# The low parts of the keys in a forgetting attention: 64 rows of the array for each head, in one tile for two heads

## The chip, the cores and the metric

The kernel runs on one core of a Trainium2 chip. The metric is the device time of one execution in microseconds (us): the median of the runs shown. A profile records one further execution, instruction by instruction, for the engines TensorE (PE, with its weight loads listed apart as PEld), VectorE (DVE), ScalarE (ACT), GpSimd (POOL) and SyncE (SP, which issues transfers).

## The reference

One layer of a hybrid encoder on 512 frames of width 1024, in float32. One input projection feeds eight heads of forgetting attention and four heads of a gated linear recurrence; both are put together by `w_out`; a cross attention over 256 memory tokens and a squared-ReLU network follow. Only the attention is touched:

```python
def fox_attention(q, k, v, log_f):
    nb = s_ // Q_BLOCK
    scale = 1.0 / math.sqrt(d_)
    F = jnp.cumsum(log_f, axis=-1)
    def block(args):
        qi, Fi, pi = args
        s = jnp.einsum('bhqd,bhkd->bhqk', qi, k).astype(jnp.float32) * scale
        s = s + Fi[..., None] - F[:, :, None, :]
        mask = pi[:, None] >= key_pos[None, :]
        s = jnp.where(mask, s, -jnp.inf)
        p = jax.nn.softmax(s, axis=-1)
        return jnp.einsum('bhqk,bhkd->bhqd', p.astype(v.dtype), v)
    out = lax.map(block, (qb, Fb, pos))
```

There are 8 heads of width 64, 512 frames and query blocks of 128 frames. Block tb sees the keys of the first (tb + 1) × 128 frames.

## The kernel before

**Numbers in two parts.** Products run in the format fp32r, which the kernel makes up for by splitting each operand into a high part (a copy in fp32r, on ScalarE) and a low part (the rest, by a subtraction on VectorE). A projection is the sum of three products: high by high, high by low, low by high (`gemm_fm`, L236 to L238, and `gemm_tm`, L249 to L251).

**Heads in pairs.** The eight heads go in four pairs p, with j = 0 or 1 inside a pair. `fox_proj(p)` (L733) projects the queries and the keys of a pair, 64 features of head 0 on partitions 0 to 63 and 64 features of head 1 on partitions 64 to 127. From the queries it makes one tile `q` for each head, in which the 64 rows of the head (the slice `r`) hold the high part and the other 64 rows (`r2`) the low part (L743, L744). From the keys it makes `kh`, with two halves by j: half j has the high part of head j on both sets of rows (L755, L756). A single product over 128 rows, q by kh, thus adds high by high and low by high. The tile `kl` has two halves too: half j holds the low part of head j on its own 64 rows (L757) and zeros on the other 64, which GpSimd writes (L748). The product q by kl over 128 rows adds high by low; the rows of the low queries meet zeros.

**Scores.** `fox_scores(p, tb)` (L924) takes both heads in turn: a bank `ps` of the pool `sc` (two buffers), the product with kh (L930), the product with kl (L931), each 128 rows by 128 stationary columns, the queries of the block, with n = 128, 256, 384 or 512 moving columns, the keys; then `fox_softmax` (L934): VectorE subtracts and takes the row's extreme (L941), ScalarE exponentiates and sums (L943), VectorE inverts and scales (L944, L945). GpSimd has prepared the bias and the mask in the tile `bi` (`fox_bias`, L915).

**The loop.** 16 steps over (pair, block) at L991. Step n transposes the probabilities of step n - 1 (`fox_T`, L953), on odd steps multiplies earlier ones by the values (`fox_out`, L969, outputs of 64 columns for each of the two heads), computes the scores of step n, has the biases of step n + 1 made and then runs a measured portion of other work, `fill.run`: the next pair's projections and the keys and values of the memory. The amounts, in microseconds, stand in `FX` (L37).

**Order.** TensorE's instructions stand in the order in which they are written out. The other engines' order is planned by the framework, with the priorities that `ahead` sets.

Two earlier pieces use other shapes on TensorE: the recurrence's products with 64 stationary columns (L629, L699) and two small transpositions, one of 33 rows (`l_soft`, L468) and four with 8 columns (`gate_rows`, L662).

Of the kernel before, what the change touches and what calls it, by code (L numbers as in the profile page):

```python
# [10 lines left out]
R = mybir.dt.float32r  # L11
U8 = mybir.dt.uint8
AF = mybir.ActivationFunctionType
ALU = mybir.AluOpType
# [3 lines left out]
S = 512  # L18
# [24 lines left out]
def emit(  # L43
# [22 lines left out]
    te, ve, ac, gp = nc.tensor, nc.vector, nc.scalar, nc.gpsimd  # L66
# [29 lines left out]
    def k4(shape, name, dt=F32):  # L96
        return k4p.tile([P] + shape, dt, tag="k4", name=name)

    def q2(name):
        return q2p.tile([P, S], R, tag="q2", name=name)  # L100

    def t3(name):
        return t3p.tile([P, S], F32, tag="t3", name=name)

    def t2(name, dt=F32, shape=(S,)):
        return t2p.tile([P] + list(shape), dt, tag="t2", name=name)
# [6 lines left out]
    def mm(name, shape=(S,)):  # L113
        return mmp.tile([P] + list(shape), F32, tag="mm", name=name)
# [4 lines left out]
    def sc(name, shape=(S,)):  # L119
        return scp.tile([P] + list(shape), F32, tag="sc", name=name)  # L120
# [4 lines left out]
    def f(a):  # L125
        return a.bitcast(F32)
# [85 lines left out]
    def next_panel():  # L212
        while len(stream) < min(state["used"] + 2, len(specs)):
            for split in load_next():
                with ahead(PW):
                    split()
        r = stream[state["used"]]
        state["used"] += 1
        return r
# [9 lines left out]
    def gemm_fm(ps, wt, col, ahi, alo, n=S, order=range(KC), begun=False):  # L229

        whi, wlo = wt
        sl = slice(col, col + P)
        for n_, k in enumerate(order):
            hi, lo = chunk(ahi, k, slice(0, n)), chunk(alo, k, slice(0, n))
            wh, wl = chunk(whi, k, sl), chunk(wlo, k, sl)
            te.matmul(ps, wh, hi, start=n_ == 0 and not begun, stop=False)  # L236
            te.matmul(ps, wh, lo, start=False, stop=False)  # L237
            te.matmul(ps, wl, hi, start=False, stop=k == order[-1])  # L238
            yield 3 * n / 2400
# [322 lines left out]
    for hp in range(2):  # L562
        wt = next_panel()
        for j in range(2):
            h = 2 * hp + j
            ps = mm(f"gq{h}")
# [115 lines left out]
    for li, m in enumerate(mlev):  # L682
# [8 lines left out]
        for hp in range(2):  # L691
# [3 lines left out]
            ps = sc(f"lv{hp}{m}", (NT, 2, w))  # L695
# [35 lines left out]
    fq, fk = {}, {}  # L731

    def fox_proj(p):  # L733
        wt = next_panel()

        fq[p] = [q2(f"q{p}{j}") for j in range(2)]
        ps = mm(f"pq{p}")
        yield from gemm_fm(ps, wt, 0, hn_hi, hn_lo)
        t = t3(f"qs{p}")
        ve.scalar_tensor_tensor(t, ps, 0.125, rbc, op0=ALU.mult, op1=ALU.mult)  # L740
        for j in range(2):
            r, r2 = slice(64 * j, 64 * j + 64), slice(64 - 64 * j, 128 - 64 * j)
            ac.activation(fq[p][j][r, :], t[r, :], AF.Copy)  # L743
            ve.tensor_tensor(fq[p][j][r2, :], t[r, :], f(fq[p][j][r, :]), ALU.subtract)  # L744
        kh, kl = k4([2, S], f"kh{p}", R), k4([2, S], f"kl{p}", R)
        fk[p] = (kh, kl)
        for j in range(2):
            gp.memset(f(kl[64 - 64 * j : 128 - 64 * j, j, :]), 0.0)  # L748
        ps = mm(f"pk{p}")
        yield from gemm_fm(ps, wt, P, hn_hi, hn_lo)  # L750
        t = t3(f"ks{p}")
        ve.tensor_tensor(t, ps, rbc, ALU.mult)
        for j in range(2):
            r, r2 = slice(64 * j, 64 * j + 64), slice(64 - 64 * j, 128 - 64 * j)
            ac.activation(kh[r, j, :], t[r, :], AF.Copy)  # L755
            ac.activation(kh[r2, j, :], t[r, :], AF.Copy)  # L756
            ve.tensor_tensor(kl[r, j, :], t[r, :], f(kh[r, j, :]), ALU.subtract)  # L757

    fill.add(fox_proj(0), "proj0")

    fill.until("gg")
# [58 lines left out]
    for c in range(NT):  # L820
# [24 lines left out]
        with ahead(P1):  # L845
            hs = sm(4, f"hs{c}")
            for h in range(4):
                j = t2(f"hj{c}{h}", F32, (P,))
# [75 lines left out]
    def fox_scores(p, tb):  # L924
        n = (tb + 1) * P
        ts_ = slice(tb * P, n)
        kh, kl = fk[p]
        for j in range(2):
            ps = sc(f"ps{2 * p + j}{tb}")
            te.matmul(ps[:, 0:n], fq[p][j][:, ts_], kh[:, j, 0:n], start=True, stop=False)  # L930
            te.matmul(ps[:, 0:n], fq[p][j][:, ts_], kl[:, j, 0:n], start=False, stop=True)  # L931
            fox_softmax((p, tb, j), ps)

    def fox_softmax(u, ps):  # L934
        p, tb, j = u
        h, n = 2 * p + j, (tb + 1) * P
        with ahead(P3):

            b = prob[u][:, 0:n]
            mx = sm(1, f"mx{h}{tb}")  # L940
            ve.tensor_tensor_reduce(out=b, in0=ps[:, 0:n], in1=b, scale=-1.0, scalar=-NEG, op0=ALU.add, op1=ALU.min, accum_out=mx)  # L941
            den = sm(1, f"dn{h}{tb}")
            ac.activation(b, b, AF.Exp, bias=mx, scale=-1.0, accum_out=den)  # L943
            ve.reciprocal(den, den)  # L944
            ve.tensor_scalar(b, b, den, None, op0=ALU.mult)  # L945
# [45 lines left out]
    for n in range(len(pairs) + 2):  # L991
        if n < len(pairs):
            p, tb = pairs[n]
            if tb == 0:
                fill.until(f"proj{p}")
                if p == 0:
                    fill.add(fox_proj(1), "proj1")
                    fill.add(proj_tm(new_fv(), WT, AF.Identity, "fv"), "fv256")
                elif p == 1:
                    fill.add(fox_proj(2), "proj2")  # L1000
                    for i in range(V0):
                        fill.add(mem_v(i))
                elif p == 2:
                    fill.until("fv256")
                    fill.add(fox_proj(3), "proj3")
                    fill.add(mem_v_wide())
                    fill.add(mem_v(3))
                    for i in range(4):
                        fill.add(mem_k(i))
# [13 lines left out]
        if n < len(pairs):  # L1023
            fox_scores(*pairs[n])
            if n + 1 < len(pairs):
                fox_biases(n + 1)
            if tb == 2 and p < 3:
                fox_rows(p + 1)
# [528 lines left out]
```

## Time and profile before

| what | value |
| --- | --- |
| median of 3 runs | 768.9 us (768.85 to 769.19) |
| profiled execution, own time | 769.28 us |
| profiled execution, span from first to last instruction | 767.5 us |
| mean granted TensorE clock | 0.998 |
| scores with kh (L930), with kl (L931) | 32 products each, 8 for each of four widths |
| fills of zeros (L748) | 8 |

In the prediction's timeline lines the columns are: start in us from the span's first instruction, duration in us (for a group, from its start to its last end, or the sum where they overlap less), engine, line, operation, the tile written and the tiles read, the shape of the array used as rows*columns, the operand's shape, and the number of instructions merged. Durations of TensorE are modelled and overlap one another; the step from one start to the next tells the pace. A bracket tells of idle time of that engine before the line and what ended it; "issue" means that no recorded event ended it. A row of the stretches gives start and end, length, and the busy time and number of instructions of each engine, then the granted clock, the share of the DMA engines and their rate. Rows that group a line show the number of instructions, the shortest, median and longest duration in ns, and the first and the last start.

### The profile page before, as it was taken

The numbers are of one execution on the slowest core, as the hardware profiler recorded it, in microseconds if no ns is written. First come the engines' busy times: TensorE is split into PE (matmuls) and PEld (weight loads), VectorE is DVE, ScalarE is ACT, GpSimd is POOL, SyncE is SP. The second block draws the span as 40 slices with busy tenths as digits, with TensorE's granted clock in tenths as the row PEclk, the third lists the DMA queues.
The fourth block names the chain that finished last, engine by engine and source line by source line (L and its number), as shares of the span: only waits on it lengthen the run. The fifth ranks groups of instructions, "written<-read, shape, count | busy, mean of one in ns | idle before, by whom it ended". The sixth has DMA issues, their size and how long they took to land.

```text
span 767.5 us, 11244 instructions
## 1 busy us (share of the span) xinstructions
PE 759.0 (99%) x4229; PEld 646.0 (84%) x4229; DVE 523.7 (68%) x849; ACT 368.7 (48%) x620; POOL 190.5 (25%) x264
## 2 busy tenths in 40 slices
PE   9999999999999999999999999999999999999996
PEld 6889888998889988888888888888888888888885
DVE  5747765576787656555548556949596868777696
ACT  5655456665666433344444244435353535342553
POOL 7207432423432025310016510101001010101123
PEclk9999999999999999999999999999999999999999
DMA  8543332232543442231113596565748475757602
GB/s 247 192 136 108 90 84 56 80 114 57 185 149 134 163 139 83 85 100 64 56 56 108 204 262 139 146 158 175 180 149 200 139 174 161 192 137 218 138 1 109
DMA packets 79831, 103.03 MB, mean 134 GB/s; under 512 B 4593, under 2 KB 58394, under 8 KB 79778
## 3 DMA queue, kind: packets, MB, share of 16 engines
q1 hardware_dynamic: 70226, 76.61, 31.1%
q0 software_dynamic: 8960, 24.67, 15.3%
q10 hardware_dynamic: 592, 1.05, 0.4%
q8 instruction: 33, 0.54, 0.3%
q14 instruction: 20, 0.16, 0.1%
HBM read 89.71 MB, written 4.21 MB: 122 GB/s over the span
## 4 chain that ended last, share of the span: by engine, by line
PE 98%; DVE 1%; ACT 1%; POOL 0%; issue 0%; DVEq 0%; ACTq 0%
PE u L238 8%; PE u L236 8%; PE u L237 8%; PE U L1371 4%; PE U L1369 4%; PE U L1370 4%; PE xq L236 2%; PE xq L237 2%; PE xw L236 2%; PE xq L238 2%; PE xw L237 2%; PE xw L238 2%; PE wo L236 2%; PE Y L1371 2%; PE wo L238 2%; PE Y L1370 2%
## 5 line engine op out<-in xcount | busy, mean ns | idle before, releaser
L175 DVE TENSOR_TENSOR wld<-wq,whd 128x1024 fp32r<-128x1024 f32 x56 | 68.6, 1226 | 25.3 <-ACT whd L171 25.2
L236 PE MATMUL u<-x_hi,whu 128*128 128x512 f32 x192 | 74.7, 389 | 0.0
L237 PE MATMUL u<-x_lo,whu 128*128 128x512 f32 x192 | 74.7, 389 | 0.0
L238 PE MATMUL u<-x_hi,wlu 128*128 128x512 f32 x192 | 74.7, 389 | 0.0
L171 ACT ACTIVATE whd<-wq 128x1024 fp32r<-128x1024 f32 x56 | 58.4, 1054 | 30.2 <-PE u L237 18.5
L171 ACT ACTIVATE whu<-wru 128x1024 fp32r<-128x1024 f32 x24 | 25.3, 1053 | 62.1 <-DMA wru<-in_w_dram 62.1
L175 DVE TENSOR_TENSOR wlu<-wru,whu 128x1024 fp32r<-128x1024 f32 x24 | 29.5, 1229 | 32.8 <-ACT whu L171 32.8
L1245 POOL DMA_DIRECT2D wq<-in_w_dram x16 | 19.4, 1242 | 129.1 <-DMA wq<-in_w_dram 117.6
L1369 PE MATMUL U<-whd,hb 128*128 128x512 f32 x120 | 46.7, 389 | 0.0
L1370 PE MATMUL U<-wld,hb 128*128 128x512 f32 x120 | 46.7, 389 | 0.0
L1371 PE MATMUL U<-whd,hb 128*128 128x512 f32 x120 | 46.7, 389 | 0.0
L1245 POOL DMA_DIRECT2D wq<-wq x16 | 14.1, 878 | 123.9 <-DVE wld L175 96.3
L237 PEld LDWEIGHTS u<-x_lo,whu 128*128 128x128 f32 x192 | 36.0, 188 | 7.5
L238 PEld LDWEIGHTS u<-x_hi,wlu 128*128 128x128 f32 x192 | 36.0, 188 | 7.5
L236 PEld LDWEIGHTS u<-x_hi,whu 128*128 128x128 f32 x192 | 36.0, 188 | 7.4
L921 POOL TENSOR_SCALAR bi<-nF,Ft 128x128 f32<-128x128 f32 (+3 forms) x32 | 20.6, 654 | 54.6 <-PE pt L953 34.5
L1308 ACT ACTIVATE sq<-ur 128x512 f32<-128x512 f32 x32 | 20.0, 627 | 26.2 <-DVE ur L1305 26.2
L1305 DVE SCALAR_TENSOR_TENSOR ur<-u,rbc 128x512 f32<-128x512 f32 x32 | 21.9, 688 | 11.5 <-PE u L238 11.5
L1370 PEld LDWEIGHTS U<-wld,hb 128*128 128x128 f32 x120 | 22.5, 188 | 4.7
L1371 PEld LDWEIGHTS U<-whd,hb 128*128 128x128 f32 x120 | 22.5, 188 | 4.7
L1369 PEld LDWEIGHTS U<-whd,hb 128*128 128x128 f32 x120 | 22.5, 188 | 4.6
L1070 ACT ACTIVATE x_hi<-hT,gv 128x512 fp32r<-128x512 f32 x16 | 11.5, 719 | 28.5 <-DVE hT L1069 28.4
(961 smaller groups left out, 2364.2 us busy)
## 6 DMA issues: line engine op xcount, KB each, us to landing
wq<-in_w_dram SPq DMA_DIRECT2D x40, 512.0 KB, 3.3
wru<-in_w_dram SPq DMA_DIRECT2D x24, 512.0 KB, 3.8
wq<-in_w_dram POOLq DMA_DIRECT2D x16, 512.0 KB, 8.2
wq<-wq POOLq DMA_DIRECT2D x16, 512.0 KB, 4.6
xTd<-xT POOLq DMA_DIRECT2D x4, 512.0 KB, 3.3
nF<-Fd POOLq DMA_DIRECT2D x8, 256.0 KB, 3.7
hT<-xTd POOLq DMA_DIRECT2D x4, 512.0 KB, 5.4
xt<-in_x_dram SPq DMA_DIRECT2D x3, 512.0 KB
```

The source lines that it names most:

```text
L171: ac.activation(hi, raw, AF.Copy)
L175: ve.tensor_tensor(lo, raw, f(hi), ALU.subtract)
L236: te.matmul(ps, wh, hi, start=n_ == 0 and not begun, stop=False)
L237: te.matmul(ps, wh, lo, start=False, stop=False)
L238: te.matmul(ps, wl, hi, start=False, stop=k == order[-1])
L921: gp.tensor_scalar(bi[:, 0:n], fF[h][:, 0:n], -1.0, Ft[:, tb, h : h + 1], op0=ALU.mult, op1=ALU.add)
L1245: gp.dma_start(raw.rearrange("p (k n) -> p k n", k=2), src, accum_op=ALU.add)
L1305: ve.scalar_tensor_tensor(u, ps, 0.0, rbc2, op0=ALU.max, op1=ALU.mult)
L1308: ac.activation(sqs[g, j][:, i, :], u, AF.Square)
L1369: te.matmul(ps, hi, whi[:, k, :], start=begin, stop=False, skip_group_check=True)
L1370: te.matmul(ps, hi, wlo[:, k, :], start=False, stop=False, skip_group_check=True)
L1371: te.matmul(ps, lo, whi[:, k, :], start=False, stop=k == 1, skip_group_check=True)
```

## The change

`kl` is now one half of its tile, 128 partitions by 512 columns, which both heads share: head 0's low part on partitions 0 to 63, head 1's on 64 to 127. The zeros and GpSimd's eight instructions for them are gone. In `fox_scores` the product with kl takes only the 64 rows of its head, of the queries' tile and of kl. The order of a call is no longer kh, kl of head 0 and kh, kl of head 1, but both banks first, then kh of head 0, kh of head 1, kl of head 0, kl of head 1, and then the two softmaxes.

```diff
-        kh, kl = k4([2, S], f"kh{p}", R), k4([2, S], f"kl{p}", R)
+        kh, kl = k4([2, S], f"kh{p}", R), k4([2, S], f"kl{p}", R)[:, 0, :]
         fk[p] = (kh, kl)
-        for j in range(2):
-            gp.memset(f(kl[64 - 64 * j : 128 - 64 * j, j, :]), 0.0)
...
-            ve.tensor_tensor(kl[r, j, :], t[r, :], f(kh[r, j, :]), ALU.subtract)
+            ve.tensor_tensor(kl[r, :], t[r, :], f(kh[r, j, :]), ALU.subtract)
...
         kh, kl = fk[p]
-        for j in range(2):
-            ps = sc(f"ps{2 * p + j}{tb}")
+        pss = [sc(f"ps{2 * p + j}{tb}") for j in range(2)]
+        for j, ps in enumerate(pss):
             te.matmul(ps[:, 0:n], fq[p][j][:, ts_], kh[:, j, 0:n], start=True, stop=False)
-            te.matmul(ps[:, 0:n], fq[p][j][:, ts_], kl[:, j, 0:n], start=False, stop=True)
+
+        for j, ps in enumerate(pss):
+            r = slice(64 * j, 64 * j + 64)
+            te.matmul(ps[:, 0:n], fq[p][j][r, ts_], kl[r, 0:n], start=False, stop=True)
+        for j, ps in enumerate(pss):
             fox_softmax((p, tb, j), ps)
```

## The prediction

> **What bounds the kernel now.** I read the page first: the span, the busy shares, the granted clock and the chain that ended last.
>
> ```profile
> span 767.5 us, 11244 instructions
> ...
> PE 759.0 (99%) x4229; PEld 646.0 (84%) x4229; DVE 523.7 (68%) x849; ACT 368.7 (48%) x620; POOL 190.5 (25%) x264
> ...
> PEclk9999999999999999999999999999999999999999
> ...
> PE 98%; DVE 1%; ACT 1%; POOL 0%; issue 0%; DVEq 0%; ACTq 0%
> ```
>
> TensorE is busy for 99% of the span at its full granted clock, and 98% of the chain lies on it. The stretch of the change is the loop over (pair, query block) at L991, from about 140 to 262 us; its busy times by engine are one row, and the list of TensorE's waits between 100 and 700 us is one other:
>
> ```profile
> 140.00:262.00 122.00, 122.00 (x900) 110.20 (x899) 87.55 (x215) 73.97 (x158) 39.38 (x82) 1.00 0.39 124
> ```
>
> ```profile
> PE pst L832 <- DVE rec L853: 0.2, 1, 0.2
> ```
>
> In 122.00 us TensorE is busy for 122.00; nobody else makes it wait. So a nanosecond that this stretch gains or loses on TensorE is a nanosecond of the kernel, and the question is only how TensorE's own order of work changes.
>
> Next the products themselves, in TensorE's timeline: three successive starts out of one call of fox_scores for each of the four widths.
>
> ```profile
> 178.30 0.27 PE L931 MATMUL ps<-kl,q 128*128 128x128 f32 x1
> 178.41 0.27 PE L930 MATMUL ps<-kh,q 128*128 128x128 f32 x1
> 178.52 0.28 PE L931 MATMUL ps<-kl,q 128*128 128x128 f32 x1
> ...
> 155.11 0.28 PE L931 MATMUL ps<-kl,q 128*128 128x256 f32 x1
> 155.22 0.28 PE L930 MATMUL ps<-kh,q 128*128 128x256 f32 x1
> 155.34 0.28 PE L931 MATMUL ps<-kl,q 128*128 128x256 f32 x1
> ...
> 161.28 0.34 PE L931 MATMUL ps<-kl,q 128*128 128x384 f32 x1
> 161.46 0.34 PE L930 MATMUL ps<-kh,q 128*128 128x384 f32 x1
> 161.63 0.33 PE L931 MATMUL ps<-kl,q 128*128 128x384 f32 x1
> ...
> 197.33 0.39 PE L931 MATMUL ps<-kl,q 128*128 128x512 f32 x1
> 197.56 0.40 PE L930 MATMUL ps<-kh,q 128*128 128x512 f32 x1
> 197.80 0.40 PE L931 MATMUL ps<-kl,q 128*128 128x512 f32 x1
> ```
>
> The column of durations overlaps and is not the cost; the step from start to start is. Halving the distance over two steps gives c = 0.11, 0.115, 0.175 and 0.235 us for 128, 256, 384 and 512 columns, and a call now costs 4c, as all four products stand in one unbroken stream. From 256 to 512 columns a step grows by 0.12 here; in the projections it grows from 0.12 (61.53 to 61.65 below) to 0.225, so by 0.105 to 0.12. I take 0.107 per 256 columns as the streaming time proper: s = 0.053, 0.107, 0.16 and 0.213. At 128 columns the step of 0.11 is twice the streaming: there the weight load sets it.
>
> **The change part by part.** Every call keeps four products with their four weight loads. What is new is the shape: two of the four use half the rows, and shapes are mixed in the stream. No 64-row product of this kind is in the trace, but there are two sets of rows near it. The first is the shape 128*64, two halves side by side in the columns (L629, L969):
>
> ```profile
> 182.60 0.39 PE L238 MATMUL pq<-hn_hi,wl12b 128*128 128x512 f32 x1
> 182.92 1.75 PE L969 MATMUL pv<-pts,fv 128*64 128x128 f32 x28
> ...
> 176.93 1.04 PE L953 MATMUL pt<-ident,bi 128*128 128x128 f32 x8
> ...
> 60.91 0.46 PE L629 MATMUL dg<-sta,mov 128*64 128x64 f32 x10
> 61.30 0.39 PE L249 MATMUL gi<-wh4a,hn_hi 128*128 128x264 f32 x1
> 61.53 0.28 PE L250 MATMUL gi<-wl4a,hn_hi 128*128 128x264 f32 x1
> 61.65 0.28 PE L251 MATMUL gi<-wh4a,hn_lo 128*128 128x264 f32 x1
> ```
>
> ```profile
> 182.92 1.51 PEld L969 LDWEIGHTS pv<-pts,fv 128*64 128x64 f32 x28 [0.35 <-issue]
> ...
> 61.30 0.19 PEld L249 LDWEIGHTS gi<-wh4a,hn_hi 128*128 128x128 f32 x1
> ```
>
> ```profile
> L629 PE MATMUL dg<-sta,mov x32: 222/222/222, 55.8 to 61.1; 128*64 128x64 f32 x32
> ```
>
> Three things are read here. First, halves run side by side: eight full products of 128 columns take 1.04 us, twenty-eight half products of the same columns only 1.75. At 0.11 apiece (1.04 less one duration of 0.27, over seven) twenty-eight in a row would need 3.2; fourteen pairs need about 0.11 × 13 + 0.27 = 1.7. Second, changing the shape stops the stream: the weights of the first half product are loaded at 182.92, 0.32 after the start of a 512-column product whose successor would have started after 0.225, and which had streamed for 0.213. So d = 0.32 - 0.213, about 0.10, passes empty, while otherwise the next weights are loaded under the running product (the list says "issue": nothing was waited for). Third, the way back costs the same: ten products of L629 end at 61.37, one takes 0.22, so the last began at 61.15; the weights of L249 come only at 61.30. Streaming 64 columns in this format takes about 0.05, so again d = 0.10; and as these weights could not be loaded ahead, L249 to L250 takes 0.23 in place of the 0.12 of the next step: the load itself, w = 0.11, lies bare.
>
> The second set is the one product that uses about half of the rows, L468 with 33, which has the rows of the change and not its columns:
>
> ```profile
> 19.54 0.40 PE L238 MATMUL gf<-hn_hi,wl0b 128*128 128x512 f32 x1
> 19.87 0.24 PE L468 MATMUL gps<-ident,rows 33*128 33x33 f32 x1
> 20.05 0.51 PE L236 MATMUL gf<-hn_hi,wh0b 128*128 128x512 f32 x1
> ```
>
> ```profile
> 19.87 0.13 PEld L468 LDWEIGHTS gps<-ident,rows 33*128 33x128 f32 x1 [0.36 <-ACT hn_hi L411]
> 20.05 0.19 PEld L236 LDWEIGHTS gf<-hn_hi,wh0b 128*128 128x128 f32 x1
> ```
>
> ```profile
> 18.77 0.69 ACT L411 ACTIVATE hn_hi<-xn,g_mix 128x512 fp32r<-128x512 f32 x1
> ```
>
> Its load comes 0.33 after the start of a 512-column product, 0.213 + 0.11, as with the half columns. The list names ScalarE as what was waited for, but that activation ended at 19.46, 0.41 earlier; so it is the change of shape. The load behind it, at 20.05, again comes with its product and not ahead of it. I therefore take the stop as given for 64 rows too, with d = 0.10.
>
> Now the new call, from kh of head 0 to the next full product: one step c to kh of head 1; its streaming s, the stop d, the bare load w; the two half products together, s plus t = 0.01 between the heads (from the fourteen pairs, which show next to nothing); the stop d and the bare load w of the fill that follows. That is c + 2s + 2d + 2w + t = c + 2s + 0.43, against 4c: a difference of 2s + 0.43 - 3c, which is +0.206, +0.299, +0.225 and +0.151 us. Together 0.88 for the four blocks of a pair, and for four pairs **+3.5 us**.
>
> Bounds. A 64-row load in this format isn't shown: if it were hidden wholly, 16 × 0.11 = 1.8 less; if the second head's load waited for the first's, 16 × 0.10 = 1.6 more. I take 0.11 each with the two side by side, because the loads of L969, two in 0.11, stand nearest. By the Trainium skill, "TensorE: Matmul & The Clock Gate", section "LDWEIGHTS (loading the stationary operand)", load time goes by columns and not by rows, so that half the rows save nothing; the sum by it is the same 3.5, and only its lower bound would fall away.
>
> The rest is at nothing, with its cover:
>
> ```profile
> L748 POOL MEMSET kl<- x8: 519/520/525, 112.8 to 198.7; 64x512 f32 x8
> L757 DVE TENSOR_TENSOR kl<-ks,kh x8: 667/684/689, 135.2 to 221.5; 64x512 fp32r<-64x512 f32 x8
> ```
>
> Eight fills of zeros leave GpSimd, 8 × 0.52 = 4.2 us of an engine busy for 39.38 of 122.00; TensorE never waits for it there. The wait for kl's buffer passes to L757, which in the eight cases begins some 22 us after the fill (135.2 against 112.8, 221.5 against 198.7). L757 keeps its size. No DMA is touched. The new order lets head 0's softmax begin later by s + d + w, 0.26 to 0.42 us, and head 1's by at most 0.1 (s + 0.21 - 2c); what is late next is the transposition at L953. The tightest block that I found has its head 1 scaled by VectorE here:
>
> ```profile
> 246.72 0.41 DVE L945 TENSOR_SCALAR bi<-bi,dn 128x384 f32<-128x384 f32 x1
> ```
>
> ```profile
> 247.72 0.87 PE L953 MATMUL pt<-ident,bi 128*128 128x128 f32 x6
> ```
>
> It ends at 247.13, and the six transpositions begin 0.6 us later, head 0's first; the delay fits in that. Without this cover it would cost TensorE up to 16 × 0.4 = 6 us, but TensorE's next block comes later too.
>
> **The rivals.**
> *The halves do not run together* (heads one behind the other in spite of separate rows). For it: side-by-side running is shown in the columns only. Each call pays c - 0.01 more: (0.635 - 0.04) × 4 = 2.4, so +5.9, 774.8 us.
>
> *No stop, and the pair costs one product: faster.* For it stands a product with only eight columns that is taken without a pause, its load coming right behind the start of the product ahead:
>
> ```profile
> 108.54 0.39 PE L266 MATMUL gg<-wh7b,hn_lo 128*128 128x512 f32 x1
> ```
>
> ```profile
> 108.55 0.53 PEld L662 LDWEIGHTS pFr<-ident,Ft 128*8 128x8 f32 x4
> ```
>
> If 64 rows went like that, each call would lose c - 0.01: 2.4 us in all, 766.5. It decides as soon as the two stops with their bare loads, 0.43 a call, fall under 3c - 2s (0.13 to 0.28). Against it is L468, which has the rows. [...]
>
> *It doesn't do what it says*: half products run as full ones with idle rows, neither stopping nor joining, 768.9. Again only L662 speaks for it.
>
> *Another order on the other engines* leaves TensorE waiting in some blocks, 1 to 3 us on top; the 0.6 us above speaks against it.
>
> **How the numbers follow.** The profiled execution took 769.28 us, 1.8 more than its span; the median of the runs is 768.9. Since the sum is a difference, I add it to the median: 768.9 + 3.5 = 772.4 (772.8 beside the profiled execution). Chances: forecast 0.66, heads one after the other 0.13, faster 0.11, nothing 0.07, other engines 0.03. The forecast's own range, with loads half hidden and rounding in the steps, is 771.3 to 773.4. The range for 8 in 10 takes in a load wholly hidden below (772.4 - 1.8 = 770.6) and the first rival above: 770.6 to 774.9; the faster case and the case of nothing stay outside with most of their 0.18. A difference of 0.2%, 1.5 us, is about what a measurement of this kernel can tell from no change: faster 0.11, same 0.07, slower 0.82.
>
> **What would show it.** In the timeline, 64*128 products of the two heads starting within 0.01 us of one another; their loads about 0.10 + s after kh of head 1; the next full load 0.10 + s after the pair; the following step longer by 0.11. "Issue" before kl's loads should be a new group of the waits, sixteen times. The stretch of 122.00 us should grow by 3.5, all others not. I am wrong if the loads of kl stand under the running kh product (then the faster rival), or if the second head's product starts a whole step later (then the slower one), or if TensorE waits at L953.

## The result and the profile after

| | before | changed |
| --- | --- | --- |
| median, 6 runs each | 769.07 us | 772.59 us |
| lowest to highest | 768.85 to 769.24 | 772.20 to 772.81 |
| profiled execution: own time, span | 769.28, 767.5 us | 772.55, 770.8 us |

The ratio is 1.0042, with a 95% interval from 1.0032 to 1.0053: slower by 3.5 us, or 0.4%.

The profile of the changed kernel looks as before, only longer:

```profile
span 770.8 us, 11232 instructions
...
PE 762.3 (99%) x4229; PEld 644.1 (84%) x4229; DVE 525.0 (68%) x849; ACT 368.2 (48%) x620; POOL 186.5 (24%) x256
...
PE 98%; DVE 1%; ACT 1%; POOL 0%; issue 0%; DVEq 0%; ACTq 0%
```

TensorE has as many instructions as before (4229) and is busy for 3.3 us more; GpSimd has eight fewer, the fills. To see where the time went, I cut both executions at the first score product and at the first product of the output projection and compare the stretches. First the kernel before, then the changed one:

```profile
0.00:148.73 148.73, 147.13 (x1070) 126.69 (x1071) 93.54 (x184) 86.97 (x170) 62.97 (x115) 1.00 0.41 125
148.73:270.79 122.06, 122.06 (x901) 110.42 (x900) 87.46 (x210) 73.37 (x150) 32.95 (x68) 1.00 0.42 134
270.79:767.50 496.71, 489.84 (x2262) 408.84 (x2260) 342.70 (x458) 208.33 (x301) 94.57 (x82) 1.00 0.50 137
```

```profile
0.00:148.58 148.58, 147.00 (x1070) 126.65 (x1071) 93.61 (x183) 86.82 (x170) 60.56 (x111) 1.00 0.42 125
148.58:274.08 125.50, 125.50 (x901) 108.71 (x900) 88.47 (x209) 73.39 (x150) 31.39 (x65) 1.00 0.42 129
274.08:770.80 496.72, 489.83 (x2262) 408.72 (x2260) 342.94 (x458) 208.02 (x302) 94.52 (x82) 1.00 0.51 137
```

The stretch with the scores grew from 122.06 to 125.50, by 3.44 us; the last one is the same to 0.01, the first differs by 0.15. That TensorE is listed as busy through the whole stretch says little, as its modelled durations overlap; but in neither kernel does the list of TensorE's waits name another engine in this stretch, and the idle time of its weight loads at the transpositions, where a late softmax would show, stayed as it was (before, then changed):

```profile
PEld pt L953 <- issue: 1.2, 7, 0.2
```

```profile
PEld pt L956 <- issue: 1.2, 7, 0.2
```

So TensorE spent the time inside its own stream, and the timeline of one call with 512 columns shows where. These are TensorE's products in the changed kernel, then its weight loads at the same place:

```profile
198.43 0.71 PE L929 MATMUL ps<-kh,q 128*128 128x512 f32 x2
199.07 0.50 PE L933 MATMUL ps<-kl,q 64*128 64x512 f32 x2
199.51 0.39 PE L249 MATMUL xv<-wh13b,meh 128*128 128x256 f32 x1
199.73 0.28 PE L250 MATMUL xv<-wl13b,meh 128*128 128x256 f32 x1
199.85 0.28 PE L251 MATMUL xv<-wh13b,mel 128*128 128x256 f32 x1
```

```profile
198.41 0.30 PEld L929 LDWEIGHTS ps<-kh,q 128*128 128x128 f32 x2
199.07 0.19 PEld L933 LDWEIGHTS ps<-kl,q 64*128 64x128 f32 x2 [0.36 <-issue]
199.51 0.19 PEld L249 LDWEIGHTS xv<-wh13b,meh 128*128 128x128 f32 x1 [0.25 <-issue]
```

The two half products stand in one row of 0.50, about as long as one of them, and their starts lie 0.003 us apart: they run side by side. But the loads of kl begin only at 199.07. The merged kh row ends at 199.14 and one such product is listed with 0.40, so the second kh began at 198.75, as the list of that moment alone shows:

```profile
198.75 0.40 PE L929 MATMUL ps<-kh,q 128*128 128x512 f32 x1
```

From 198.75 to 199.07 is 0.32, the same as at the half columns of before: the kh product streams for 0.213 (the prediction's s), and 0.11 more passes before the load. The way out has the same stop: the load of L249, with "issue" as the only reason, comes 0.44 after kl's, which is the bare load, the streaming and the stop, 0.11 + 0.213 + 0.10, to about 0.01; and the step behind it is 0.22 where the next is 0.12. "Issue" before kl's loads is a new entry in the list of waits, the largest of the weight queue:

```profile
PEld ps L933 <- issue: 2.5, 8, 0.4
```

### The profile page after: what moved, and what is told of

Same layout as the page of the kernel before. It is cut to its first block, busy times and chain, and to the rows that moved or that the text cites. A ratio compares the mean times of both kernels' runs of the same rounds, so it can differ in the third digit from the quotient of the medians.

```text
span 770.8 us, 11232 instructions
## 1 busy us (share of the span) xinstructions
PE 762.3 (99%) x4229; PEld 644.1 (84%) x4229; DVE 525.0 (68%) x849; ACT 368.2 (48%) x620; POOL 186.5 (24%) x256
## 4 chain that ended last, share of the span: by engine, by line
PE 98%; DVE 1%; ACT 1%; POOL 0%; issue 0%; DVEq 0%; ACTq 0%
PE u L237 8%; PE u L236 8%; PE u L238 8%; PE U L1373 4%; PE U L1372 4%; PE U L1374 4%; PE xq L236 2%; PE xq L237 2%; PE xw L237 2%; PE xw L236 2%; PE xq L238 2%; PE wo L236 2%; PE wo L237 2%; PE xw L238 2%; PE Y L1372 2%; PE Y L1373 2%
## 5 line engine op out<-in xcount | busy, mean ns | idle before, releaser
L1328 ACT ACTIVATE hb<-s 128x512 fp32r<-128x512 f32 x24 | 15.0, 630 | 20.7 <-PE U L1374 13.6
```

## The experiments

All of them keep the rest of the kernel. Each was timed in turns with the kernel before; the ratio is to that.

### The order alone

```diff
-        for j in range(2):
-            ps = sc(f"ps{2 * p + j}{tb}")
+        pss = [sc(f"ps{2 * p + j}{tb}") for j in range(2)]
+        for j, ps in enumerate(pss):
             te.matmul(ps[:, 0:n], fq[p][j][:, ts_], kh[:, j, 0:n], start=True, stop=False)
+        for j, ps in enumerate(pss):
             te.matmul(ps[:, 0:n], fq[p][j][:, ts_], kl[:, j, 0:n], start=False, stop=True)
-            fox_softmax((p, tb, j), ps)
+        for j, ps in enumerate(pss):
+            fox_softmax((p, tb, j), ps)
```

> All four products over 128 rows with the zeros in kl, as before, but in the new order: kh, kh, kl, kl, then both softmaxes. My theory (the whole loss lies in the change of the array's shape): 769.1 us, no difference from before. Rival (the order itself costs, because head 0's softmax starts later and TensorE then waits in the next step): something between 769.1 and the 772.6 of the changed kernel, with waits of TensorE's weight loads at the transpositions.

Measured: 769.69 us, ratio 1.0001 (0.9992 to 1.0010). No difference. Its profile has TensorE's numbers of before to the last digit:

```profile
span 767.5 us, 11245 instructions
...
PE 759.0 (99%) x4229; PEld 646.0 (84%) x4229; DVE 524.6 (68%) x849; ACT 368.8 (48%) x620; POOL 190.4 (25%) x264
```

The later softmax of head 0 costs nothing. So the loss does not lie in the order; the 64 rows and the fills of zeros are left.

### The fills of zeros kept

```diff
-        kh, kl = k4([2, S], f"kh{p}", R), k4([2, S], f"kl{p}", R)[:, 0, :]
+        kh, kl = k4([2, S], f"kh{p}", R), k4([2, S], f"kl{p}", R)
+        for j in range(2):
+            gp.memset(f(kl[64 - 64 * j : 128 - 64 * j, 1, :]), 0.0)
+        kl = kl[:, 0, :]
```

> The changed kernel, with GpSimd's eight fills of zeros kept (they go to the unused half of kl's tile). My theory: 772.6 us, unchanged, since TensorE never waited for GpSimd there. Rival (the fills that left gave back a part of the loss): up to 4.2 us more, 776.8.

Measured: 772.71 us, ratio 1.0043 (1.0028 to 1.0058), as the changed kernel. The 4 us of work that left GpSimd gave nothing back, so the 64 rows are left.

### The old order with 64 rows

```diff
-        pss = [sc(f"ps{2 * p + j}{tb}") for j in range(2)]
-        for j, ps in enumerate(pss):
+        for j in range(2):
+            ps = sc(f"ps{2 * p + j}{tb}")
+            r = slice(64 * j, 64 * j + 64)
             te.matmul(ps[:, 0:n], fq[p][j][:, ts_], kh[:, j, 0:n], start=True, stop=False)
-
-        for j, ps in enumerate(pss):
-            r = slice(64 * j, 64 * j + 64)
             te.matmul(ps[:, 0:n], fq[p][j][r, ts_], kl[r, 0:n], start=False, stop=True)
-        for j, ps in enumerate(pss):
             fox_softmax((p, tb, j), ps)
```

> The 64-row products, but in the old order kh, kl of head 0, kh, kl of head 1: four changes of shape in a call and no two half products side by side. My theory (each change of shape costs the stop of 0.10 and a bare load of 0.11, four of them): a call takes 4s + 0.84 in place of 4c, in all +11.8, 780.9 us. Rival (the loss belongs to the half products as such, a slower pace of 64 rows, or to the call as a whole, and not to each change of shape): about 772.6, or 2.4 more for the pairs that no longer run together, 775.0.

Measured: 781.23 us, ratio 1.0151 (1.0134 to 1.0168). With four changes of shape in a call the loss is 11.8 us, against 3.5 with two. TensorE's timeline of this kernel, a call with 512 columns:

```profile
172.30 0.47 PE L930 MATMUL ps<-kh,q 128*128 128x512 f32 x1
172.70 0.50 PE L931 MATMUL ps<-kl,q 64*128 64x512 f32 x1
173.13 0.50 PE L930 MATMUL ps<-kh,q 128*128 128x512 f32 x1
173.56 0.49 PE L931 MATMUL ps<-kl,q 64*128 64x512 f32 x1
173.99 0.39 PE L249 MATMUL fv<-wh11b,hn_hi 128*128 128x256 f32 x1
```

Behind a change of shape every product takes a step of 0.43, full or half, where the unbroken stream took 0.235: s + d + w = 0.213 + 0.10 + 0.11. The price is on each change and not on the half rows.

### Both heads on the same rows

```diff
         for j, ps in enumerate(pss):
-            r = slice(64 * j, 64 * j + 64)
+            r = slice(0, 64)
             te.matmul(ps[:, 0:n], fq[p][j][r, ts_], kl[r, 0:n], start=False, stop=True)
```

> The changed kernel, but head 1's product with kl takes rows 0 to 63 as head 0's does (so head 1's low part is not computed rightly; the amount of work is the same). Two half products on the same rows cannot run side by side. My theory (they do run side by side in the changed kernel): the second starts a whole step after the first, 0.635 - 0.04 more for the four widths, 2.4 in all, 775.0 us. Rival (they were one behind the other all along and the starts 0.004 apart are only their issue): 772.6 us, unchanged.

Measured: 775.02 us, ratio 1.0073 (1.0058 to 1.0088), 2.4 us more than the changed kernel. In its timeline the two half products now take 0.73 together, a whole step of 0.23 over the 0.50 of one:

```profile
171.46 0.73 PE L933 MATMUL ps<-kl,q 64*128 64x512 f32 x2
172.12 0.39 PE L249 MATMUL fv<-wh11b,hn_hi 128*128 128x256 f32 x1
```

So in the changed kernel they do run side by side, and that gains what was expected of it: 2.4 us. It is less than the two changes cost.

This run also gives the price of a change without the pair. In the old order, too, the half products run one behind the other, but the shape changes four times in a call and not twice: 781.23 less 775.02 is 6.2 us for 32 more changes, 0.19 each (the terms of the prediction give 5.9).

### More than one pair for a change

The low products of a call are taken two or three times in a row, once with half rows and once over 128 rows (the low part is then added two or three times). The edit on half rows, with 2 or 3 for N; the one on full rows repeats the full products in the same way, in the order of the first experiment. The kernel with two pairs on half rows has the second pair written out as a line of its own, L936:

```diff
+        for i in range(N):
-        for j, ps in enumerate(pss):
-            r = slice(64 * j, 64 * j + 64)
-            te.matmul(ps[:, 0:n], fq[p][j][r, ts_], kl[r, 0:n], start=False, stop=True)
+            for j, ps in enumerate(pss):
+                r = slice(64 * j, 64 * j + 64)
+                te.matmul(ps[:, 0:n], fq[p][j][r, ts_], kl[r, 0:n], start=False, stop=i == N - 1)
```

> The changed kernel, with each pair of low products taken twice in a row (kl, kl, kl, kl: the low part is added twice). It tells what one more pair costs once the shape has been changed. My theory (the stop and the bare load are paid for the change only; inside one shape the next loads go under the running pair): one ordinary step c more in each call, 0.635 x 4 = 2.5, 775.1 us. Rival 1 (the next pair's weights cannot be loaded under the running pair on the same rows): s + w each, 3.9 more, 776.5. Rival 2 (every pair stops the stream): s + d + w each, 5.5 more, 778.1.

> Four low products in a call, over 128 rows with the zeros: two more steps than before, 2 x 0.635 x 4 = 5.1, 774.2 us, by any theory of mine. Beside the 775.2 of two pairs of half rows this puts the point from which the half rows pay between two and three pairs for one change of shape.

> The changed kernel with each pair of low products taken three times in a row (the low part is added three times). My theory (two changes of shape are paid once for a call, every further pair costs one step c): two more steps than the changed kernel, 2 x 0.635 x 4 = 5.1, 777.7 us. Rival (further pairs pay a stop or a bare load too): 780.4 or more.

> The same six low products in a call, over 128 rows with the zeros in kl: no change of shape, one step for each. Four more steps than before, 4 x 0.635 x 4 = 10.2, 779.3 us; so with three pairs for one change the half rows should be the faster by some 1.6 us, if my theory holds, and the slower by some 1 us or more if the rival does.

| pairs in a call | half rows | full rows |
| --- | --- | --- |
| 1 | 772.59 | 769.07 (before) |
| 2 | 775.21, ratio 1.0078 (1.0060 to 1.0096) | 774.46, ratio 1.0066 (1.0049 to 1.0083) |
| 3 | 777.97, ratio 1.0113 (1.0098 to 1.0128) | 780.08, ratio 1.0140 (1.0125 to 1.0155) |

A further pair costs 2.6 and 2.8 us on half rows, 5.4 and 5.6 on full rows; 2.5 and 5.1 were expected, so that the full rows with three pairs came out 0.8 us above the time expected. The rivals of the second pair, 776.5 and 778.1 us, lie above all its runs (775.05 to 775.37), that of the third, 780.4, above all of those with three (777.24 to 778.34). In the timeline of the kernel with two pairs, the second pair's loads (L936) come 0.11 behind the first's, long before its products, and the second pair starts 0.34 after the first, the bare load of 0.11 and one step:

```profile
171.29 0.50 PE L933 MATMUL ps<-kl,q 64*128 64x512 f32 x2
171.63 0.40 PE L936 MATMUL ps<-kl,q 64*128 64x512 f32 x2
171.96 0.39 PE L249 MATMUL fv<-wh11b,hn_hi 128*128 128x256 f32 x1
```

```profile
171.29 0.19 PEld L933 LDWEIGHTS ps<-kl,q 64*128 64x128 f32 x2 [0.37 <-issue]
171.40 0.19 PEld L936 LDWEIGHTS ps<-kl,q 64*128 64x128 f32 x2
171.95 0.19 PEld L249 LDWEIGHTS fv<-wh11b,hn_hi 128*128 128x128 f32 x1 [0.36 <-issue]
```

Inside one shape loading ahead works as in the full stream. With two pairs the intervals of the two ratios overlap (the two kernels were timed at different times, so the ratios are what to compare); with three pairs these intervals just touch, at 1.0128 and 1.0125, but the two kernels were timed together and all runs of the half rows lie below all of the full rows (779.42 to 780.36): the point from which half rows pay is near two pairs and under three. The kernel has one pair in a call.

### Beside the other half shape

```diff
-        if n >= 3 and n % 2 == 1:
+        if n == len(pairs) + 1:
             for step in pairs[n - 3 : n - 1]:
                 fox_out(*step)
...
             fox_scores(*pairs[n])
+            if n >= 3 and n % 2 == 1:
+                for step in pairs[n - 3 : n - 1]:
+                    fox_out(*step)
```

> The changed kernel, with the products with the values (L972, the half columns) taken right behind the half-row pair on seven of the odd steps, so that the stream goes full, half rows, half columns, full in place of full, half columns, full, half rows, full: three changes of shape for four. My theory (every change costs one stop and one bare load, also between two half shapes): seven times a stop and a short load less, 7 x 0.15 = 1.1, 771.5 us. Rival 1 (going between two half shapes costs as much as going through the full one): 772.6. Rival 2 (between two half shapes nothing stops): 770.5.

Measured: 771.57 us, ratio 1.0030 (1.0019 to 1.0041), 1.0 less than the changed kernel. Seven changes fewer, at 0.15 each: the theory's 771.5. All its runs (771.10 to 772.00) lie between the two rivals, but by so little (its ratio's interval overlaps that of the changed kernel, from 1.0032) that the time alone would not decide. Its weight loads do: going from half rows to half columns stops the stream once, as the load of L972 comes 0.42 after kl's, again w + s + d:

```profile
169.96 0.19 PEld L933 LDWEIGHTS ps<-kl,q 64*128 64x128 f32 x2 [0.36 <-issue]
170.38 0.64 PEld L972 LDWEIGHTS pv<-pts,fv 128*64 128x64 f32 x12 [0.24 <-issue]
171.19 0.19 PEld L249 LDWEIGHTS fv<-wh11b,hn_hi 128*128 128x128 f32 x1 [0.17 <-issue]
```

It still loses to the kernel before. No run beat that one. Three pairs for a change would need the low products of several blocks together and so, as it seems, more banks for scores than the two of `sc`; this was not tried.

## Why the prediction was right

- **TensorE bound, so its stream decides.** Right: the stretch of the scores grew by 3.44 us where the span grew by 3.3, and TensorE waited for no other engine there, nor longer at the transpositions.
- **The stop, d = 0.10, for 64 rows as for 64 columns and 33 rows.** Right, and shown in two ways: kl's load 0.32 after the second kh at 512 columns, and 11.8 us for twice as many changes, of which 2.4 are the pair that came apart.
- **The bare load, w = 0.11, on both sides.** Right: steps of 0.22 against 0.12 behind a call, and 0.43 for every product behind a change in the old order. Half the rows do not load faster; the lower end of the range, 770.6, allowed for a load that is hidden wholly. The Trainium skill, "TensorE: Matmul & The Clock Gate", section "LDWEIGHTS (loading the stationary operand)", has load time go by columns and not by rows. The trace agrees: loads of kl over 64 rows are listed with 0.183 us, those of kh over 128 with 0.19. One of the prediction's two reasons for 0.11 doesn't hold, though. The loads of L969, "two in 0.11", run under their products, which themselves step by 0.11 a pair; where such loads lie bare, in front of the first pair, the second pair starts 0.16 after it in place of 0.11, so that only about 0.05 is theirs, for 64 columns. What carried over is the bare load of L249, which has 128 columns as kl's has.
- **The two heads side by side.** Right: with both on the same rows it is 2.4 us slower, the price that the prediction gave this rival.
- **Order and fills at nothing.** Right: 769.69 and 772.71 us.
- **The sum, 0.43 a call against 3c - 2s.** 3.5 predicted, 3.52 by the medians, 3.44 in the stretch. By width it was less exact than the sum. Take the time from the second product of a call to the second behind the call. At 512 columns the timeline of before has 0.82 (197.33 to 198.15), that of after 0.98 (198.75 to 199.73):

```profile
198.03 0.27 PE L249 MATMUL xv<-wh13b,meh 128*128 128x256 f32 x1
198.15 0.28 PE L250 MATMUL xv<-wl13b,meh 128*128 128x256 f32 x1
```

  Over all sixteen calls the differences are on average 0.18, 0.28, 0.22 and 0.17 us for 128, 256, 384 and 512 columns, against 0.21, 0.30, 0.23 and 0.15 predicted. The weight loads tell why. From kl's load to the next full load it takes 0.44 at 512 columns, as above, and 0.25 at 128:

```profile
179.26 0.19 PEld L933 LDWEIGHTS ps<-kl,q 64*128 64x128 f32 x2
179.51 0.19 PEld L249 LDWEIGHTS fv<-wh11b,hn_hi 128*128 128x128 f32 x1
```

  On average it is 0.26, 0.31, 0.37 and 0.43 for the four widths: 0.20 at every width for the stop and the bare load together, and a streaming that grows by 0.117 per 256 columns. The prediction had 0.21 and 0.107; it had seen a growth of 0.12 in the scores' own steps and took the smaller one of the projections. The first is a little too much and the second a little too small, so that the nearly exact sum owes something to luck.
- **"Issue" sixteen times.** Not so: the list shows eight, for the calls with 384 and 512 columns. In the narrow ones the listed duration of the load before (0.19) hides most of the wait: 0.07 us of idle time are left at 128 columns and 0.13 at 256, and the list names no such short ones. The stop is there all the same, as the 0.20 at every width shows.
- **The rival without a stop.** It rested on the transpositions with eight columns, which indeed run without one, in the changed kernel too (their first load starts 0.004 us behind the start of the full product ahead). They were a poor neighbour for the change: 33 rows were the nearer one. Why eight columns go without a stop is not shown. The Trainium skill, "TensorE: Matmul & The Clock Gate", Part 3, has products in different row tiles start about 4 ns apart and run concurrently. The trace agrees: the two heads' products start 3 to 4 ns apart in all sixteen calls.

## What to carry to other kernels

Before products are made smaller to run side by side, count the changes of the array's shape that they bring: here each took about 0.1 us of empty array and a weight load of up to 0.11 that could not go ahead, some 0.2 in a stream whose products take 0.11 to 0.235. Half rows pay when several pairs follow one another for each change, here about even with two pairs and 2.1 us faster with three; and they cost less beside other small products than in the middle of full ones. A profile that has a product near the new shape in it can show this price before the change is made: look at the start of its weight load against the product ahead of it. Not every small product will do: here 64 columns and 33 rows showed the stop, eight columns did not.

## What the runs showed of the hardware that was not expected

Going from half rows straight to half columns costs one change and not two, nor none (771.57 us). And each change leaves a mark that is easily missed: TensorE's products cover the whole stretch in the list, before (122.06 of 122.06) and after (125.50 of 125.50), because their modelled durations overlap; only the weight queue shows the gap, and the list of waits names it, as "issue", only where it is long enough: for eight of the sixteen calls.
